# Attention masks in a two-block transformer kernel: one VectorE operation per head in place of identity products on TensorE

## The chip, the core and the metric

The kernel runs on one core of a Trainium2 chip. A core has five engines with an instruction queue each: TensorE (PE, matrix products; its weight loads are shown apart as PEld), VectorE (DVE), ScalarE (ACT), GpSimd (POOL) and SyncE (SP, which issues most transfers). Products land in PSUM; everything else works on SBUF. The metric is the device time of one execution in microseconds (us).

## What is computed

The reference is two models in sequence, each of depth 2, on one sequence of 256 tokens with 1024 channels, all float32. Each layer of the first has two feed-forward halves around a mixer with dilated-window attention (12 heads in three dilation groups) and stick-breaking attention (4 heads). Each layer of the second has a mixer of four branches (an attention with compressed, selected and windowed parts, a gated convolution, a pooling branch and a sliding-window attention with sinks), gates, and a feed-forward part. The change is in the softmax of the attentions. Cut to that:

```
# dilated window: key j is visible to query i if 0 <= i-j <= w and (i-j) % d == 0
s = einsum(q, k) * 64**-0.5
s = where(valid, s, -inf)
m = max(s);  p = exp(s - m);  o = (p @ v) / sum(p)

# banded attention (second model): window of 128 with sinks, or causal without
s = where(mask, einsum(q, k) * 64**-0.5, -1e30)
m = maximum(max(s), sink);  e = exp(s - m)
p = e / (sum(e) + exp(sink - m));  o = p @ v
```

## The kernel before

The 256 tokens are two tiles of 128 rows (t = 0, 1). All large products are done in three passes of a high and a low half of each operand; the low half of each weight chunk is made by VectorE (`wl`, line L111) and the high half by ScalarE (`wh`, L110), from chunks that SyncE loads. The products of such a chunk with activations stand in helper lines L184 to L186.

The program is written in order, layer by layer, but a scheduler places the instructions: it takes them by priority and by planned costs, puts independent ones into the gaps, and fixes one order per engine before the kernel runs. So gate products of the same mixer (`gate`, results `gt` at L955) are found between the attention's instructions, and the steps of the convolution (`conformer`, L911 and L914, 30 taps on each of four channel blocks) run on VectorE among the attention's.

First block, `attend1`: for each tile, heads are taken in pairs of `js`, and each keeps the scores of its dilation groups side by side in one PSUM bank of up to 512 columns (one group of 384 columns for t = 0, two of 512 and 256 for t = 1). A mask bank starts with a product of the identity (`identb`, bf16) and the additive mask `dilm` (0 or -1e30), L436; the score products of queries and keys (`qk`) of 64 rows each, L443, add to it. VectorE takes the maximum over the bank (L446), `probs` scales it (L454), ScalarE takes the exponential out of PSUM into an SBUF tile `e` with the sum beside it (L458), VectorE divides (L466), TensorE transposes (`transposed`, L155), and the value products follow (L488). The stick-breaking part keeps its own identity product (L499) in both kernels.

Second block, `attn`: called for the sliding-window attention (`window` true, with sinks) and twice for the causal one, for each tile and layer, always for 8 heads. For t = 0 a bank holds 4 heads of 128 columns, for t = 1 2 heads of 256. Identity products with the mask `swm` start each bank: L567 for t = 0, L569 for the window at t = 1, L571 for the causal case at t = 1, where only the second half of the columns needs one. Score products L578, then:

```
V.tensor_reduce(mx[:, sl], pv, op=OP.max, axis=AX.X)      # L584
V.tensor_scalar(ng[:, sl], mx[:, sl], -0.125, None, ...)  # L586, or L588 and L589 with sinks
S.activation(ev[:, i], pv[:, i], AF.Exp, bias=ng[...], scale=0.125, accum_out=dn[...])  # L593, per head
V.reciprocal(f[:, hh], dn[:, hh])                         # L602
V.tensor_tensor(ev, ev, f[...], op=OP.mult)               # L606
```

`turned` transposes the probabilities (L155) and copies them (L612, L614); L625 multiplies by the values. PSUM has two rings of four banks, `lin` and `aux`; scores, transposes and value products share `aux`. The SBUF tiles `e` come from a ring of 18. The masks are loaded once by GpSimd's queue at the start (`load_consts`).

Of the kernel before, what the change touches and what calls it, by code (L numbers as in the profile page):

```python
# [10 lines left out]
BF16 = mybir.dt.bfloat16  # L11
AF = mybir.ActivationFunctionType
# [13 lines left out]
def body(tc, ctx, I, C, out, upto=99):  # L26
# [35 lines left out]
    def const(name, shape, dt=F32):  # L62
        t = cp.tile(list(shape), dt, tag=name, name=name)
        pending.append((t, C[name]))
        return t
# [17 lines left out]
    G.memset(half, -0.5)  # L83
    dilm = [const(f"dilm{t}", [P, 3, (t + 1) * P], BF16) for t in range(2)]
    sbm = const("sbm", [P, P], BF16)
    swm = const("swm", [P, 2 * P], BF16)
    rope1 = [const(f"rope1_{t}", [P, 32]) for t in range(2)]
    rope2 = [const(f"rope2_{t}", [P, 128]) for t in range(2)]
    ntri = const("ntri", [P, P])
# [151 lines left out]
    def kouter(xts, w, nk, done, late=0):  # L241
# [3 lines left out]
        for b in range(2):  # L245
# [16 lines left out]
                go(1, c)  # L262
            done(1, b, ps[1])

    def square(src):

        junk = unit("junk", BF16, 1024)[:, :src.shape[-1]]
        m = stat()
        S.activation(junk, src, AF.Square, scale=1.0 / 32.0, accum_out=m)
        return m  # L270
# [127 lines left out]
    def attend1(qkn, vs):  # L398
        QT = [None, None]
        oTs = []  # L400
        for t in range(2):
# [19 lines left out]
            def qk(h, isk, tt):  # L421
                b = (h // 2) + (6 if isk else 0)
                o = (h % 2) * 64
                return QT[tt][b // 8][o:o + 64, (b % 8) * P:(b % 8 + 1) * P]
# [4 lines left out]
            def scores(js):  # L429

                r = [([], stat(4), stat(4)) for _ in js]
                for gi, gs in enumerate(groups):
                    n = len(gs) * nk * P
                    pss = [aux_ps()[:, :n] for _ in js]
                    for ps in pss:
                        nc.tensor.matmul(ps, identb, dilm[t][:, gs[0]:gs[-1] + 1, :].rearrange("p g k -> p (g k)"),  # L436
                                         start=True, stop=False)
                    for gg in gs:
                        for kt in range(nk):
                            c0 = ((gg - gs[0]) * nk + kt) * P  # L440
                            for ps, j in zip(pss, js):
                                h = gg * 4 + j
                                nc.tensor.matmul(ps[:, c0:c0 + P], qk(h, False, t), qk(h, True, kt), start=False,  # L443
                                                 stop=(gg == gs[-1] and kt == nk - 1))
                    for ps, (ps_l, mx, sm) in zip(pss, r):
                        V.tensor_reduce(mx[:, gi:gi + 1], ps, op=OP.max, axis=AX.X)  # L446
                        ps_l.append(ps)
                return r

            def probs(j, ps_l, mx, sm):  # L450

                if len(groups) == 2:
                    V.tensor_tensor(mx[:, 0:1], mx[:, 0:1], mx[:, 1:2], op=OP.max)
                V.tensor_scalar(mx[:, 2:3], mx[:, 0:1], -0.125, None, op0=OP.mult)  # L454
                es = []
                for gi, gs in enumerate(groups):
                    e = unit("e")[:, :len(gs) * nk * P]
                    S.activation(e, ps_l[gi], AF.Exp, bias=mx[:, 2:3], scale=0.125, accum_out=sm[:, gi:gi + 1])  # L458
                    es.append(e)
                if len(groups) == 2:  # L460
                    V.tensor_add(sm[:, 0:1], sm[:, 0:1], sm[:, 1:2])
                V.reciprocal(sm[:, 2:3], sm[:, 0:1])
                pts = []
                for gi, (gs, e) in enumerate(zip(groups, es)):
                    n = len(gs) * nk * P
                    V.tensor_scalar(e, e, sm[:, 2:3], None, op0=OP.mult)  # L466
                    pt = transposed(blocks(e, n // P))
                    u = unit("pt")[:, :n]
                    if gi == 0:
                        V.tensor_copy(u, pt)  # L470
                    else:
                        S.activation(u, pt, AF.Copy)
                    for gg in gs:
                        for kt in range(nk):
                            c0 = ((gg - gs[0]) * nk + kt) * P
                            h = gg * 4 + j
                            pts.append((vs[kt][:, h * 64:h * 64 + 64], u[:, c0:c0 + P]))
                return pts
# [73 lines left out]
    def attn(t, qT, kTf, vf, window, po, first, last, gate=None, sink=None):  # L552


        nk = t + 1
        per = 4 if t == 0 else 2
        mx, ng, dn, f = stat(8), stat(8), stat(8), stat(8)
        es = {}

        def scores(h0):  # L560

            n = per * nk * P
            pvs = []
            for _ in range(2):
                pv = aux_ps()[:, :n].rearrange("p (h k) -> p h k", h=per)
                if t == 0:
                    nc.tensor.matmul(pv, identb, swm[:, None, P:].to_broadcast([P, per, P]), start=True, stop=False)  # L567
                elif window:
                    nc.tensor.matmul(pv, identb, swm[:, None, :].to_broadcast([P, per, 2 * P]), start=True, stop=False)  # L569
                else:  # L570
                    nc.tensor.matmul(pv[:, :, P:], identb, swm[:, None, P:].to_broadcast([P, per, P]), start=True, stop=False)  # L571
                pvs.append(pv)
            for i in range(per):
                for kt in range(nk):
                    for par, pv in enumerate(pvs):
                        h = h0 + 2 * i + par
                        q_ = qT[par * 64:par * 64 + 64, (h // 2) * P:(h // 2 + 1) * P]
                        nc.tensor.matmul(pv[:, i, kt * P:(kt + 1) * P], q_, kTf(kt, h), start=False,  # L578
                                         stop=(i == per - 1 and kt == nk - 1))
            r = []  # L580
            for par, pv in enumerate(pvs):
                hs = list(range(h0 + par, h0 + 2 * per, 2))
                sl = slice(h0 + par, h0 + par + 2 * per - 1, 2)
                V.tensor_reduce(mx[:, sl], pv, op=OP.max, axis=AX.X)  # L584
                if sink is None:
                    V.tensor_scalar(ng[:, sl], mx[:, sl], -0.125, None, op0=OP.mult)  # L586
                else:
                    V.scalar_tensor_tensor(mx[:, sl], mx[:, sl], 0.125, sink[:, sl], op0=OP.mult, op1=OP.max)  # L588
                    V.tensor_scalar(ng[:, sl], mx[:, sl], -1.0, None, op0=OP.mult)  # L589
                e = unit("e")[:, :n]  # L590
                ev = e.rearrange("p (h k) -> p h k", h=per)
                for i, h in enumerate(hs):
                    S.activation(ev[:, i], pv[:, i], AF.Exp, bias=ng[:, h:h + 1], scale=0.125, accum_out=dn[:, h:h + 1])  # L593
                r.append((sl, ev))
                for i, h in enumerate(hs):
                    es[h] = ev[:, i]
            hh = slice(h0, h0 + 2 * per)
            if sink is not None:
                V.tensor_tensor(f[:, hh], sink[:, hh], ng[:, hh], op=OP.add)
                S.activation(f[:, hh], f[:, hh], AF.Exp)  # L600
                V.tensor_add(dn[:, hh], dn[:, hh], f[:, hh])
            V.reciprocal(f[:, hh], dn[:, hh])  # L602
            if gate is not None:
                V.tensor_tensor(f[:, hh], f[:, hh], gate[:, hh], op=OP.mult)
            for sl, ev in r:
                V.tensor_tensor(ev, ev, f[:, sl][:, :, None].to_broadcast([P, per, nk * P]), op=OP.mult)  # L606

        def turned(g, kt):
            u = unit("pt")
            pt = transposed([es[4 * g + r][:, kt * P:(kt + 1) * P] for r in range(4)])  # L610
            if (g + kt) % 2 == 0:
                V.tensor_copy(u, pt)  # L612
            else:
                S.activation(u, pt, AF.Copy)  # L614
            return u

        us = {}
        for h0 in range(0, 8, 2 * per):
            scores(h0)
        for kt in range(nk):  # L620
            for g in range(2):
                us[g, kt] = turned(g, kt)
        for kt in range(nk):
            for g in range(2):
                nc.tensor.matmul(po[g * 64:(g + 1) * 64], vf(kt, g), us[g, kt], start=first and kt == 0,  # L625
                                 stop=last and kt == nk - 1)
# [495 lines left out]
def constants():  # L1122
# [23 lines left out]
        c[f"cmpm{t}"] = np.concatenate([add, ok], axis=1).astype(f)  # L1146
    c["sbm"] = np.where(q < k, 0.0, NEG).astype(f)
    c["ntri"] = np.where(q >= k, -1.0, 0.0).astype(f)
    c["swm"] = np.concatenate([np.where(k > q, 0.0, NEG), np.where(k <= q, 0.0, NEG)], axis=1).astype(f)
    row = np.arange(P)  # L1150
    c["hsel"] = ((2 * ((row // 16) % 4) + row // 64)[:, None] == np.array([0, 4, 1, 5, 2, 6, 3, 7])[None, :]).astype(f)
    cnt = np.stack([np.minimum(np.arange(T) + 1, w) for w in (2, 4, 8, 16)]).astype(f)
# [54 lines left out]
```

## Time and profile before

| | |
|---|---|
| median of 3 runs | 2146.33 us |
| lowest, highest | 2140.66, 2147.63 us |
| profiled execution | 2142.42 us |
| span of its trace | 2140.7 us |
| mean granted TensorE clock | 0.997 of full speed |

The rows of the trace below come from the one profiled execution. Its time is the device time; the span is from the first to the last instruction of the trace. A group of instructions shows its count, its busy time, the mean of one, and the idle time of the engine just ahead of it. A matmul's duration runs from its start to its last result, so neighbouring ones overlap; the distance from start to start says how long the engine is taken.

### The profile page before, as it was taken

The page shows a single profiled execution, that of the slowest core. Times are in us where ns is not written, and L with a number is a line of the kernel's source. Part 1 is how long each engine was busy: PE and PEld are TensorE (multiplying, and loading weights), DVE is VectorE, ACT ScalarE, POOL GpSimd, SP SyncE. Part 2 cuts the span into 40 slices and gives each one's busy share as a digit, 9 for nine tenths or more (in the row PEclk, how much of TensorE's full clock was granted, in tenths as well). Part 3 has the DMA queues.
Part 4 walks back from the last instruction along what each step waited for, and adds up shares of the span by engine and source line. Part 5 has one row for each costly group of instructions (what it writes and reads, how often), then busy time and mean ns, then how long its engine had stood idle before and what let it go on. Part 6 is the DMA issues. An engine that isn't in the chain of part 4 may idle for free.

```text
span 2140.7 us, 30396 instructions
## 1 busy us (share of the span) xinstructions
PE 2103.5 (98%) x11520; PEld 1760.2 (82%) x11520; DVE 1576.4 (74%) x2439; ACT 1159.0 (54%) x1786; POOL 34.2 (2%) x47
## 2 busy tenths in 40 slices
PE   7999999999999999999999999999999999999998
PEld 6888877888888887788887877779987877788997
DVE  6875466786677555577757999678966899777983
ACT  5554556554555455555545655556655564446652
POOL 0000000000000000000000000000000000000000
PEclk9999999999999999999999999999999999999999
DMA  8666534666666654366666743356656644265653
GB/s 257 202 188 184 191 117 145 190 189 195 189 188 187 190 187 142 121 185 187 187 189 186 225 129 118 121 183 201 187 191 190 213 149 139 88 195 177 187 177 119
DMA packets 250818, 373.81 MB, mean 175 GB/s; under 512 B 14768, under 2 KB 123696, under 8 KB 250672
## 3 DMA queue, kind: packets, MB, share of 16 engines
q1 hardware_dynamic: 250096, 371.48, 56.8%
q8 instruction: 90, 1.47, 0.3%
q0 software_dynamic: 576, 0.39, 0.1%
q14 instruction: 56, 0.46, 0.1%
HBM read 371.17 MB, written 1.05 MB: 174 GB/s over the span
## 4 chain that ended last, share of the span: by engine, by line
PE 88%; DVE 7%; ACT 1%; issue 1%; DMA 1%; POOL 1%; SPq 0%; POOLq 0%; DVEq 0%; ACTq 0%
PE lin L186 15%; PE lin L185 15%; PE lin L184 15%; PE lin L218 15%; PE lin L219 8%; PE aux L155 3%; PE lin L205 3%; PE lin L206 3%; PE lin L204 3%; DVE cy L914 2%; DVE wl L111 2%; PE aux L625 1%; PE aux L578 1%; DMA raw<-in_w_in_dram 1%; PE aux L443 1%
## 5 line engine op out<-in xcount | busy, mean ns | idle before, releaser
L111 DVE TENSOR_TENSOR wl<-raw,wh 128x1024 fp32r<-128x1024 f32 (+1 forms) x688 | 835.1, 1217 | 393.4 <-ACT wh L110 386.1
L110 ACT ACTIVATE wh<-raw 128x1024 fp32r<-128x1024 f32 (+1 forms) x688 | 722.2, 1055 | 522.6 <-PE lin L186 277.3
L218 PE MATMUL lin<-x,wh 128*128 128x512 f32 x1408 | 494.8, 396 | 0.0
L219 PE MATMUL lin<-x,wl 128*128 128x256 f32 x1408 | 394.4, 280 | 0.0
L185 PE MATMUL lin<-wl,x 128*128 128x512 f32 (+2 forms) x896 | 348.2, 389 | 1.9 <-DVE wl L111 1.9
L184 PE MATMUL lin<-wh,x 128*128 128x512 f32 (+2 forms) x896 | 349.0, 390 | 0.0
L186 PE MATMUL lin<-wh,x 128*128 128x512 f32 (+2 forms) x896 | 346.7, 388 | 1.0 <-DVE rs L1105 0.8
L218 PEld LDWEIGHTS lin<-x,wh 128*128 128x128 f32 x1408 | 264.7, 188 | 62.4
L219 PEld LDWEIGHTS lin<-x,wl 128*128 128x128 f32 x1408 | 266.0, 189 | 0.5 <-DVE wl L111 0.4
L186 PEld LDWEIGHTS lin<-wh,x 128*128 128x128 f32 x896 | 168.7, 188 | 40.8 <-issue 5.2
L185 PEld LDWEIGHTS lin<-wl,x 128*128 128x128 f32 x896 | 168.7, 188 | 37.3 <-DVE wl L111 3.0
L184 PEld LDWEIGHTS lin<-wh,x 128*128 128x128 f32 x896 | 168.6, 188 | 36.5 <-issue 4.3
L186 PE MATMUL lin<-wh,lo 128*128 128x512 f32 x480 | 188.6, 393 | 0.4 <-DVE lo L147 0.4
L184 PE MATMUL lin<-wh,hi 128*128 128x512 f32 x480 | 187.3, 390 | 0.0
L185 PE MATMUL lin<-wl,hi 128*128 128x512 f32 x480 | 187.0, 390 | 0.0
L205 PE MATMUL lin<-x,wh 128*128 128x256 f32 x576 | 163.2, 283 | 0.0
L206 PE MATMUL lin<-x,wl 128*128 128x256 f32 x576 | 163.0, 283 | 0.0
L204 PE MATMUL lin<-x,wh 128*128 128x256 f32 x576 | 163.0, 283 | 0.0
L205 PEld LDWEIGHTS lin<-x,wh 128*128 128x128 f32 x576 | 110.6, 192 | 0.1
L204 PEld LDWEIGHTS lin<-x,wh 128*128 128x128 f32 x576 | 110.6, 192 | 0.1
L206 PEld LDWEIGHTS lin<-x,wl 128*128 128x128 f32 x576 | 110.6, 192 | 0.0
L225 ACT ACTIVATE su<-lin 128x256 f32<-128x256 f32 x176 | 65.4, 375 | 76.5 <-PE lin L219 76.5
(308 smaller groups left out, 2662.2 us busy)
## 6 DMA issues: line engine op xcount, KB each, us to landing
raw<-in_ffn_w_up_dram SPq DMA_DIRECT2D x168, 512.0 KB, 3.9
raw<-in_ffn_w_down_dram SPq DMA_DIRECT2D x132, 512.0 KB, 3.7
raw<-in_w_in_dram SPq DMA_DIRECT2D x132, 512.0 KB, 4.3
raw<-in_ffn_w_gate_dram SPq DMA_DIRECT2D x88, 512.0 KB, 3.8
raw<-in_w_gate_dram SPq DMA_DIRECT2D x64, 512.0 KB, 4.1
raw<-in_w_branch_dram SPq DMA_DIRECT2D x32, 512.0 KB, 4.2
raw<-in_w_out_dram SPq DMA_DIRECT2D x16, 512.0 KB, 4.5
raw<-in_nsa_cmp_w_dram SPq DMA_DIRECT2D x16, 512.0 KB, 4.5
```

The costliest lines, as they stand in the source:

```text
L110: S.activation(wh, raw, AF.Copy)
L111: V.tensor_sub(wl, raw, wh.bitcast(F32))
L155: nc.tensor.transpose(p[:, i * P:(i + 1) * P], s, ident)
L184: nc.tensor.matmul(ps, xt.h[k], w[0], start=start, stop=False)
L185: nc.tensor.matmul(ps, xt.h[k], w[1], start=False, stop=False)
L186: nc.tensor.matmul(ps, xt.l[k], w[0], start=False, stop=stop)
L204: nc.tensor.matmul(o, wh, xh, start=k == 0 and i % 2 == 0, stop=False)
L205: nc.tensor.matmul(o, wh, xl, start=False, stop=False)
L206: nc.tensor.matmul(o, wl, xh, start=False, stop=k == 7 and i % 2 == 1)
L218: nc.tensor.matmul(o, wh, x, start=k == 0, stop=False)
L219: nc.tensor.matmul(o[:, :T], wl, x[:, :T], start=False, stop=k == 7)
L225: S.activation(u[:, i * T:(i + 1) * T], p[:, T:], AF.Copy)
```

## The change

The masks are no longer added on TensorE. The first score product of a bank now starts it. A new helper `masked` adds the mask to the scores, writes the sum to the SBUF tile `e`, and takes the maximum, in one VectorE operation: per bank in `attend1`, per head in `attn`. The exponential then reads `e` and writes it in place. `swm` doubles to four blocks of 128 columns (earlier keys, own keys, zeros, own keys), so that each case finds its mask as one slice.

```
-    swm = const("swm", [P, 2 * P], BF16)
+    swm = const("swm", [P, 4 * P], BF16)
+    def masked(out, ps, mask, mx):
+        V.tensor_tensor_reduce(out, ps, mask, 1.0, NEG, OP.add, OP.max, mx)
...
-                    for ps in pss:
-                        nc.tensor.matmul(ps, identb, dilm[t][:, gs[0]:gs[-1] + 1, :].rearrange("p g k -> p (g k)"),
-                                         start=True, stop=False)
...
-                                nc.tensor.matmul(ps[:, c0:c0 + P], qk(h, False, t), qk(h, True, kt), start=False,
-                                                 stop=(gg == gs[-1] and kt == nk - 1))
+                                nc.tensor.matmul(ps[:, c0:c0 + P], qk(h, False, t), qk(h, True, kt),
+                                                 start=(gg == gs[0] and kt == 0), stop=(gg == gs[-1] and kt == nk - 1))
                     for ps, (ps_l, mx, sm) in zip(pss, r):
-                        V.tensor_reduce(mx[:, gi:gi + 1], ps, op=OP.max, axis=AX.X)
-                        ps_l.append(ps)
+                        e = unit("e")[:, :n]
+                        masked(e, ps, dilm[t][:, gs[0]:gs[-1] + 1, :].rearrange("p g k -> p (g k)"), mx[:, gi:gi + 1])
+                        ps_l.append(e)
...
-                    e = unit("e")[:, :len(gs) * nk * P]
-                    S.activation(e, ps_l[gi], AF.Exp, bias=mx[:, 2:3], scale=0.125, accum_out=sm[:, gi:gi + 1])
+                for gi, e in enumerate(es):
+                    S.activation(e, e, AF.Exp, bias=mx[:, 2:3], scale=0.125, accum_out=sm[:, gi:gi + 1])
...
+        mask = swm[:, 3 * P:] if t == 0 else swm[:, :2 * P] if window else swm[:, 2 * P:]
...
-                if t == 0:
-                    nc.tensor.matmul(pv, identb, swm[:, None, P:].to_broadcast([P, per, P]), start=True, stop=False)
-                elif window:
-                    nc.tensor.matmul(pv, identb, swm[:, None, :].to_broadcast([P, per, 2 * P]), start=True, stop=False)
-                else:
-                    nc.tensor.matmul(pv[:, :, P:], identb, swm[:, None, P:].to_broadcast([P, per, P]), start=True, stop=False)
...
-                        nc.tensor.matmul(pv[:, i, kt * P:(kt + 1) * P], q_, kTf(kt, h), start=False,
+                        nc.tensor.matmul(pv[:, i, kt * P:(kt + 1) * P], q_, kTf(kt, h), start=(i == 0 and kt == 0),
                                          stop=(i == per - 1 and kt == nk - 1))
...
-                V.tensor_reduce(mx[:, sl], pv, op=OP.max, axis=AX.X)
+                e = unit("e")[:, :n]
+                ev = e.rearrange("p (h k) -> p h k", h=per)
+                for i, h in enumerate(hs):
+                    masked(ev[:, i], pv[:, i], mask, mx[:, h:h + 1])
...
-                    S.activation(ev[:, i], pv[:, i], AF.Exp, bias=ng[:, h:h + 1], scale=0.125, accum_out=dn[:, h:h + 1])
+                    S.activation(ev[:, i], ev[:, i], AF.Exp, bias=ng[:, h:h + 1], scale=0.125, accum_out=dn[:, h:h + 1])
```

## Rows read from the trace of the kernel before

**Rows 1.** The page: busy time by engine, and VectorE in 40 slices.

```profile
PE 2103.5 (98%) x11520; PEld 1760.2 (82%) x11520; DVE 1576.4 (74%) x2439; ACT 1159.0 (54%) x1786; POOL 34.2 (2%) x47
...
DVE  6875466786677555577757999678966899777983
```

**Rows 2.** Busy time by stretch; columns: length, PE, PEld, DVE, ACT, POOL, clock, DMA.

```profile
840.00:905.00 65.00, 64.17 (x377) 48.52 (x374) 35.97 (x71) 39.23 (x64) 0.00 (x0) 1.00 0.37 110
...
1230.00:1260.00 30.00, 28.76 (x166) 21.27 (x165) 29.61 (x74) 18.60 (x50) 0.00 (x0) 1.00 0.36 118
...
1230.00:1350.00 120.00, 118.36 (x651) 86.19 (x649) 109.06 (x247) 63.64 (x156) 0.00 (x0) 1.00 0.37 114
...
1200.00:1204.00 4.00, 3.34 (x11) 2.95 (x12) 4.00 (x8) 3.58 (x8) 0.00 (x0) 0.57 0.66 174
```

**Rows 3.** Waits of PE and PEld, whole run: total us, times, longest.

```profile
PE aux L155 <- DVE e L606: 2.6, 6, 0.8
...
PEld aux L443 <- issue: 3.5, 14, 0.4
...
PEld aux L578 <- issue: 2.5, 10, 0.4
...
PEld L436 <- issue: 1.8, 8, 0.3
```

**Rows 4.** The masks' tiles: count, ns min/median/max, first and last start, forms.

```profile
L436 PE MATMUL aux<-dilm,identb x24: 273/331/389, 269.1 to 871.9; 128*128 128x384 bf16 x8, 128*128 128x512 bf16 x8, 128*128 128x256 bf16 x8
...
L571 PE MATMUL aux<-swm,identb x16: 272/282/283, 1317.9 to 1843.1; 128*128 128x256 bf16 x16
L567 PE MATMUL aux<-swm,identb x12: 379/379/390, 1231.4 to 1798.2; 128*128 128x512 bf16 x12
L569 PE MATMUL aux<-swm,identb x8: 379/379/389, 1250.1 to 1756.0; 128*128 128x512 bf16 x8
```

**Rows 5.** Timeline of PE: start, us from first start to last end, instructions merged.

```profile
276.14 0.50 PE L436 MATMUL aux<-dilm,identb 128*128 128x384 bf16 x2
...
285.05 0.38 PE L499 MATMUL aux<-sbm,identb 128*128 128x256 bf16 x2
...
1200.66 1.12 PE L155 MATMUL aux<-ident,kd 128*128 128x128 f32 x4 [2.21 <-DVE kd L550]
...
1231.38 0.59 PE L567 MATMUL aux<-swm,identb 128*128 128x512 bf16 x2
```

**Rows 6.** Groups by shape on ACT: busy us, mean ns, idle before and its releasers.

```profile
L146 ACT ACTIVATE hi<-su 128x512 fp32r<-128x512 f32 x44 | 27.1, 616 | 1.6 <-DVE su L343 1.6
...
L146 ACT ACTIVATE x<-aux 128x512 fp32r<-128x512 f32 x40 | 23.7, 596 | 11.9 <-PE aux L155 11.4
...
L593 ACT ACTIVATION_READ_ACCUMULATOR e<-aux,st 128x1 f32 x96 | 20.2, 210 | 0.0
...
L593 ACT ACTIVATE e<-aux,st 128x128 f32<-128x128 f32 (+1 forms) x96 | 39.1, 426 | 32.8 <-DVE st L586 25.3 <-DVE st L588 7.5
```

**Rows 7.** Timeline of DVE in second-block attention.

```profile
1283.99 1.28 DVE L584 TENSOR_REDUCE st<-aux 128x4 f32<-128x512 f32 x2
1285.19 0.16 DVE L586 TENSOR_SCALAR st<-st 128x4 f32<-128x4 f32 x1
1285.26 0.47 DVE L914 SCALAR_TENSOR_TENSOR cy<-cT,pm,cy 128x245 f32<-128x245 f32 x1
...
1315.38 0.29 DVE L895 TENSOR_TENSOR sc<-sc,st 128x128 f32<-128x128 f32 x1
1315.59 0.84 DVE L914 SCALAR_TENSOR_TENSOR cy<-cT,pm,cy 128x230 f32<-128x230 f32 x2
```

**Rows 8.** The convolution's split result: who writes it, who reads it.

```profile
L184 PE MATMUL lin<-wh,bhi x32: 389/389/393, 1402.2 to 1918.6; 128*128 128x512 f32 x32
...
L150 DVE SCALAR_TENSOR_TENSOR blo<-cy,bhi x2: 1224/1225/1226, 1370.1 to 1874.2; 128x1024 fp32r<-128x1024 f32 x2
```

**Rows 9.** DMA issues: KB each, median us to landing.

```profile
swm<-c_swm_dram POOLq DMA_DIRECT2D x1, 64.0 KB, 8.8
```

More of the change, by code (lines that the diff above doesn't have):

```diff
@@ L454, in probs @@
                 V.tensor_scalar(mx[:, 2:3], mx[:, 0:1], -0.125, None, op0=OP.mult)
-                es = []
-                for gi, gs in enumerate(groups):
-                    e = unit("e")[:, :len(gs) * nk * P]
-                    S.activation(e, ps_l[gi], AF.Exp, bias=mx[:, 2:3], scale=0.125, accum_out=sm[:, gi:gi + 1])
-                    es.append(e)
+                es = ps_l
+                for gi, e in enumerate(es):
+                    S.activation(e, e, AF.Exp, bias=mx[:, 2:3], scale=0.125, accum_out=sm[:, gi:gi + 1])
                 if len(groups) == 2:
@@ L564, in scores @@
             for _ in range(2):
-                pv = aux_ps()[:, :n].rearrange("p (h k) -> p h k", h=per)
-                if t == 0:
-                    nc.tensor.matmul(pv, identb, swm[:, None, P:].to_broadcast([P, per, P]), start=True, stop=False)
-                elif window:
-                    nc.tensor.matmul(pv, identb, swm[:, None, :].to_broadcast([P, per, 2 * P]), start=True, stop=False)
-                else:
-                    nc.tensor.matmul(pv[:, :, P:], identb, swm[:, None, P:].to_broadcast([P, per, P]), start=True, stop=False)
-                pvs.append(pv)
+                pvs.append(aux_ps()[:, :n].rearrange("p (h k) -> p h k", h=per))
             for i in range(per):
@@ L589, in scores @@
                     V.tensor_scalar(ng[:, sl], mx[:, sl], -1.0, None, op0=OP.mult)
-                e = unit("e")[:, :n]
-                ev = e.rearrange("p (h k) -> p h k", h=per)
                 for i, h in enumerate(hs):
-                    S.activation(ev[:, i], pv[:, i], AF.Exp, bias=ng[:, h:h + 1], scale=0.125, accum_out=dn[:, h:h + 1])
+                    S.activation(ev[:, i], ev[:, i], AF.Exp, bias=ng[:, h:h + 1], scale=0.125, accum_out=dn[:, h:h + 1])
                 r.append((sl, ev))
@@ L1148, in constants @@
     c["ntri"] = np.where(q >= k, -1.0, 0.0).astype(f)
-    c["swm"] = np.concatenate([np.where(k > q, 0.0, NEG), np.where(k <= q, 0.0, NEG)], axis=1).astype(f)
+    c["swm"] = np.concatenate([np.where(k > q, 0.0, NEG), np.where(k <= q, 0.0, NEG), np.zeros((P, P)),
+                               np.where(k <= q, 0.0, NEG)], axis=1).astype(f)
     row = np.arange(P)
```

## The prediction

> **What bounds the kernel now.** I read the page first. TensorE (PE) is busy 98% of the span, VectorE (DVE) 74% in the mean, but at 9 tenths in the slices around 1180 to 1340 us and 1710 to 1820 us [rows 1]. So the mean hides two regimes, and the busy time by stretch shows them: in first-block attention (840 to 905 us) PE is busy 64.17 of 65 us while DVE is free nearly half the time; in second-block attention (1230 to 1350 us) PE is busy 118.36 of 120 us at full clock and DVE 109.06, and between 1230 and 1260 us DVE has only 0.39 us free [rows 2]. Last, the list of waits: over the whole run PE waited for DVE's scaled probabilities (L606) 2.6 us, in 6 times [rows 3]. PE ends last everywhere near the change, because the scheduler fills the softmax latency with gate products. An instruction less on PE is therefore time less, as long as DVE, which also makes PE's low weight halves (L111), is not made late.
>
> **What leaves PE.** 60 identity products go: 8 + 12 + 8 of 512 columns, 8 of 384, and 8 + 16 of 256 [rows 4]. Their durations overlap with their neighbours', so I price them by pairs. Two of 512 columns take 0.59 us where one takes 0.38: 0.21 us each. Two of 384 take 0.50 against 0.33: 0.17. Two of 256 (the same product in L499, which stays) take 0.38 against 0.28: 0.10 [rows 4, 5]. Sum: 28 x 0.21 + 8 x 0.17 + 24 x 0.10 = 5.9 + 1.4 + 2.4 = 9.7 us. To that come gaps: the weight loads stood 1.8 us ahead of L436, 3.5 us ahead of L443 and 2.5 us ahead of L578 with nothing but issue in the way [rows 3]. The 1.8 us go with L436. Of the other 6.0 us the part remains where a score block still follows transposes or value products; I let up to half go. So PE saves 9.7 us by streaming alone and 9.7 + 1.8 + 3.0 = 14.5 at most; I take 11, nearer to the part that rows show directly. That these products merely stood in waits is a rival below.
>
> **What comes to DVE.** 36 maxima over several heads (L584, 512 columns) become one operation per head: in each layer three attentions of 8 heads in each of two tiles, 48 a layer and 96 in all, 48 of 128 and 48 of 256 columns. The 24 maxima of the first block (L446) become 24 operations of the same width. A DVE operation that writes both a sum and its maximum is in no row, so I bound it. What counts is start to start: two 512-column maxima hold DVE from 1283.99 to 1285.19 us, 0.60 each; a two-input operation of 128 columns is followed after 0.21 us; on the line between them 256 columns hold it 0.34 [rows 7]. Below, the maximum comes with the stream at no price: 48 x 0.21 + 48 x 0.34 - 36 x 0.60 = 10.1 + 16.3 - 21.6 = +4.8 us, and nothing in the first block. Above, the maximum is read out as ScalarE reads out its sum, in an instruction of 0.21 us [rows 6]: 120 x 0.21 = 25.2 more, +30.0 us. The nearest DVE row is the tiny operation, which the next one follows after 0.07 us (1285.19 to 1285.26) [rows 7]; with 0.08 to be a little above it the sum is 4.8 + 120 x 0.08 = +14.4 us: 2.4 + 48 x 0.08 = 6.2 in each layer of the second block and 1 in each of the first. I take this one.
>
> The cover for the 6.2 us is the convolution (L914), which DVE runs among the attention work: its split result is written from 1370.1 us and PE first loads it at 1402.2 us [rows 8], about 30 us of slack, and 10.94 of the 120 us are free besides [rows 2]. So I cost the throughput at nothing. If that cover is gone, or the convolution stands ahead of the new work in DVE's fixed order, the sum falls on PE (first rival).
>
> Latency is the second part. In a first-tile attention the maxima of both head groups took 2 x 0.60 = 1.2 us; eight operations of 0.21 + 0.08 take 2.3, so 1.1 later. In a second-tile step four of 0.42 take 1.7, so 0.5 later. What is late next is the exponential (L593), then L602, L606 and the transposes of L155 on PE, and behind those the gate products in PE's order. Most of it is filled with gate products; at the six places where PE waits for L606 already [rows 3] I add 0.3 to 0.4 us each: 2 us lost.
>
> **The rest.** ScalarE's 120 exponentials read SBUF instead of PSUM. The nearest rows, a 512-column copy from SBUF at 616 ns and one from PSUM at 596 [rows 6], put it at 0.02 us each, 2.4 us: nothing, hidden by the 32.8 us that ScalarE waits for DVE ahead of L593 [rows 6]; without that cover it would be 2.4 us on PE's transposes. Score banks come free after the DVE operation instead of after the exponentials, and the SBUF tile of the exponentials, one of 18, is taken as much earlier: both nothing, since no row has PE waiting long for either. The mask load on GpSimd's queue doubles from 64 KB, which landed in 8.8 us [rows 9], and is the last on that queue, 1200 us ahead of its reader at 1231 us [rows 5]: nothing, and some 9 us if it had to be waited for.
>
> [...]
>
> **Sum.** PE -11, waits +2: -9 us. The profiled execution took 2142.42 us, its span 2140.7 (the table above); -9 gives 2133.4. It lies 3.9 us under the median of the runs shown, 2146.33, and from that the same -9 gives 2137.
>
> **Rivals.**
>
> *DVE becomes the bound of attention (slower).* For it: 0.39 us free from 1230 to 1260 us [rows 2], and DVE's order is fixed when the kernel is built; if the new operation is longer than was planned for, convolution pieces and L111 behind it slip, and PE, also in order, waits at the next transpose. Against it: the slack of the convolution, and 120 operations are few beside 2439 [rows 1]. With nothing absorbed the sum is -11 + 14.4 = +3 us at my price and -11 + 30 = +19 at the upper one; it decides (+6.4) from 17.4 us that reach PE, that is from a read-out of 0.105 us with nothing absorbed. [...] 2149 to 2165 us; chance 0.15.
>
> *The products filled waits (no change).* For it: at 1231.38 us a mask pair runs directly behind the transposes of the queries [rows 5], whose copy to SBUF the score products need, so it may cost nothing there. If half the streamed time merely turns into waits, or DVE's 6 us a layer reach PE in part, -3 us remains: 2143 (2140 to 2150). Against it: PE has gate products at hand in almost every such gap. Chance 0.27.
>
> *More comes back.* Every gap that could go does, and no wait is added: -14.5 us, 2132 (2128 to 2132). Chance 0.08.
>
> **How the numbers follow.** The forecast, 2137 us with a range of its own of 2132 to 2140, has 0.50. The range 2128 to 2150 leaves out most of the first rival's 0.15 and little else. A difference under 0.3% (6.4 us) is about what a measurement of this kernel can't tell from no change. Faster by more: 0.48 of the forecast and 0.08 of the last case, 0.56. Within: 0.02 + 0.27 and a little of the first rival, 0.30. Slower: 0.14.
>
> **What would show it.** Right: PE has 60 matmuls fewer and its busy time falls by about 10 us; DVE's busy time rises by 10 to 30 us; the convolution ends later, still before 1402 us; PE's waits for L606 and L111 stay under 10 us. Wrong: DVE operations that hold the engine 0.5 us or more for 128 columns; a granted clock under 0.9 in attention; PE waiting for L111 or L606 by more than 10 us in all; or gate products in another order, so that time moves where the change is not.

## The result, and the profile after

The changed kernel takes 2118.72 us (median of 4 runs, 2113.38 to 2119.26); the kernel before took 2145.01 us beside it (4 runs, 2140.66 to 2147.63). The ratio is 0.9874, with an interval of 0.985 to 0.9897: 26 us faster. The forecast was 2137 us, with a range of 2128 to 2150: the sign was right, the size was not, and the time lies 9 us below the range.

The profiled execution took 2119.26 us, its span 2117.5. The page of the changed kernel, busy time by engine:

```profile
PE 2081.5 (98%) x11460; PEld 1752.2 (83%) x11460; DVE 1580.3 (75%) x2619; ACT 1164.2 (55%) x1786; POOL 34.2 (2%) x47
...
DVE  6875566777687555577857899878976899977983
```

Against [rows 1] PE has its 60 matmuls fewer and is busy 22.0 us less; its idle time stays where it was (2140.7 - 2103.5 = 37.2 us, now 36.0). So the 23 us of span came out of PE's busy time, and that is twice what the removed products were priced at. DVE has 180 instructions more and is busy only 3.9 us longer.

Where it happened is read by stage. A stage lies between two tiny GpSimd operations (`st<-st,half`), which the trace of every kernel here has at the same places of the program: the two attention stages of the first block and the two mixer layers of the second. Busy time in these four, before (columns as in [rows 2]):

```profile
203.50:386.40 182.90, 181.85 (x947) 143.88 (x947) 108.79 (x175) 98.50 (x144) 2.01 (x2) 1.00 0.49 152
757.50:940.50 183.00, 181.95 (x947) 143.88 (x947) 108.81 (x175) 98.37 (x144) 2.01 (x2) 1.00 0.49 153
1136.30:1433.30 297.00, 290.24 (x1506) 229.87 (x1505) 245.37 (x450) 157.79 (x285) 1.40 (x4) 0.99 0.52 162
1638.10:1938.40 300.30, 294.07 (x1520) 232.58 (x1519) 246.99 (x451) 158.36 (x286) 1.38 (x4) 0.99 0.52 162
```

and after:

```profile
206.40:385.30 178.90, 178.14 (x935) 142.23 (x934) 108.95 (x187) 98.48 (x145) 2.03 (x3) 1.00 0.49 156
758.50:937.50 179.00, 178.21 (x935) 142.30 (x935) 108.92 (x187) 98.52 (x144) 2.01 (x2) 1.00 0.50 156
1133.40:1421.20 287.80, 282.00 (x1488) 227.61 (x1487) 246.95 (x528) 159.87 (x286) 1.44 (x5) 0.99 0.55 167
1626.00:1915.60 289.60, 283.56 (x1502) 228.94 (x1501) 248.58 (x529) 160.59 (x286) 1.38 (x4) 1.00 0.54 168
```

The two first stages shorten by 4.0 us each, the two layers by 9.2 and 10.7: 28 us. The rest of the span, whose work is the same, took 1177.4 us before and 1182.3 after (1178 to 1182 in the kernels of the experiments), which is why the spans differ by 23 only. DVE's busy column hardly moves in any of the four. From here on kernels are compared by these four lengths, beside their medians.

**What the new operation costs DVE.** Groups by shape, the changed kernel (`aux` is a PSUM bank: VectorE reads the scores there itself, as ScalarE did before [rows 6], so not everything but the products works on SBUF):

```profile
L267 DVE CUSTOM_DVE_ANT_0 e<-aux,swm 128x256 f32<-128x256 f32 x48 | 18.5, 419 | 0.0
...
L267 DVE CUSTOM_DVE_ANT_0 e<-aux,swm 128x128 f32<-128x128 f32 x48 | 11.2, 289 | 0.2
...
L267 DVE DVE_READ_ACCUMULATOR2_ANT st<- 128x1 f32 x120 | 10.1, 85 | 0.0
```

The maximum is read out in an instruction of its own, 85 ns long, 120 of them: near the 0.08 us that the prediction took. But the timeline of DVE shows that it costs nothing:

```profile
1230.59 0.28 DVE L267 CUSTOM_DVE_ANT_0 e<-aux,swm 128x128 f32<-128x128 f32 x1
1230.80 0.08 DVE L267 DVE_READ_ACCUMULATOR2_ANT st<- 128x1 f32 x1
1230.80 0.28 DVE L267 CUSTOM_DVE_ANT_0 e<-aux,swm 128x128 f32<-128x128 f32 x1
1231.01 0.08 DVE L267 DVE_READ_ACCUMULATOR2_ANT st<- 128x1 f32 x1
...
1315.12 0.42 DVE L267 CUSTOM_DVE_ANT_0 e<-aux,swm 128x256 f32<-128x256 f32 x1
1315.46 0.09 DVE L267 DVE_READ_ACCUMULATOR2_ANT st<- 128x1 f32 x1
1315.46 0.42 DVE L267 CUSTOM_DVE_ANT_0 e<-aux,swm 128x256 f32<-128x256 f32 x1
```

The read-out starts at the same instant as the next operation. Start to start an operation of 128 columns takes 0.21 us with its read-out and one of 256 columns 0.34: the prediction's lower bound (+4.8 us in all), not its choice (+14.4). The 0.34 - 0.21 = 0.13 us for 128 columns more leave about 0.08 us of each operation that does not grow with the columns, an estimate from these two distances.

**What PE waits for.** List of waits, PE alone, the changed kernel:

```profile
PE aux L155 <- DVE e L601: 2.5, 2, 1.3
PE lin L185 <- DVE wl L111: 1.5, 2, 0.8
...
PE aux L572 <- DVE st L267: 0.8, 2, 0.4
PE aux L155 <- DVE e L466: 0.7, 2, 0.4
```

L601 is L606 of before: 2.5 us in 2 times, where it was 2.6 in 6 [rows 3]. The 2 us that were added there for latency didn't come; two other waits for DVE that the list of before doesn't have, for the new operation ahead of the next score products (L572) and for the scaled probabilities of the first block (L466), take 1.5 us together.

**Work that was not touched.** The value products of the second block (L625 before, L620 after) are the same 36 products, each with two records in the trace. Their group before:

```profile
L625 PE MATMUL aux<-pt,vv 128*64 128x512 f32 x72 | 25.5, 616 | 0.2 <-ACT pt L614 0.2
```

and after:

```profile
L620 PE MATMUL aux<-pt,vv 128*64 128x512 f32 x72 | 19.3, 612 | 0.0
```

The timeline of PE at the end of a layer, before:

```profile
1344.34 1.07 PE L625 MATMUL aux<-pt,vv 128*64 128x512 f32 x2
1345.35 0.50 PE L186 MATMUL lin<-wh,x 128*128 128x512 f32 x1
...
1347.81 1.07 PE L625 MATMUL aux<-pt,vv 128*64 128x512 f32 x2 [0.18 <-ACT pt L614]
1348.81 0.51 PE L186 MATMUL lin<-wh,x 128*128 128x512 f32 x1
...
1349.47 1.08 PE L625 MATMUL aux<-pt,vv 128*64 128x512 f32 x4
```

and after:

```profile
1339.74 2.06 PE L620 MATMUL aux<-pt,vv 128*64 128x512 f32 x8
```

The products of the two head groups, each with weights of 128*64, write the two halves of 64 rows of one result (`po`). One alone (x2) takes 1.07 us; two that stand next to each other (x4) take 1.08 us: they run side by side. In the kernel before, gate products and transposes (from L186 on) stood between the two products of this pair, and three pairs of nine in each layer are broken in such a way; after, none is. Six pairs at 1.0 us are the 6.2 us between 25.5 and 19.3. The change doesn't touch these products, and the prediction names them only as neighbours of the score products.

**The clock.** Near the end of the second layer of the kernel before, PE waited 0.46 us, and behind it the granted clock fell; the place in the timeline of PE, and busy time by stretch:

```profile
1865.73 0.84 PE L934 MATMUL aux<-ident,st 128*128 128x128 f32 x4 [0.46 <-POOL st L931]
```

```profile
1866.00:1870.00 4.00, 4.00 (x14) 3.24 (x14) 3.33 (x7) 0.79 (x1) 0.00 (x0) 0.57 0.00 0
```

With a granted clock of 0.57, (1 - 0.57) x 4 = 1.7 us of these 4 us are lost against full clock (an estimate from the two figures). At the same place of the program the changed kernel holds full clock, 1.00:

```profile
1847.00:1855.00 8.00, 8.00 (x47) 6.89 (x46) 6.33 (x11) 2.28 (x3) 0.70 (x1) 1.00 0.41 133
```

### The profile page after: what moved, and what is told of

It reads as the page before. It is cut to its first block, busy times and chain, and to the rows that moved or that the text cites. A ratio compares the mean times of both kernels' runs of the same rounds, so it can differ in the third digit from the quotient of the medians.

```text
span 2117.5 us, 30460 instructions
## 1 busy us (share of the span) xinstructions
PE 2081.5 (98%) x11460; PEld 1752.2 (83%) x11460; DVE 1580.3 (75%) x2619; ACT 1164.2 (55%) x1786; POOL 34.2 (2%) x47
## 4 chain that ended last, share of the span: by engine, by line
PE 89%; DVE 6%; ACT 2%; issue 1%; DMA 1%; POOL 0%; SPq 0%; POOLq 0%; DVEq 0%; ACTq 0%
PE lin L186 16%; PE lin L185 16%; PE lin L218 16%; PE lin L184 16%; PE lin L219 8%; PE aux L155 3%; PE lin L206 3%; PE lin L205 3%; PE lin L204 3%; DVE wl L111 2%; DVE cy L909 1%; ACT wh L110 1%; PE aux L620 1%; DMA raw<-in_w_in_dram 1%; PE aux L572 1%
## 5 line engine op out<-in xcount | busy, mean ns | idle before, releaser
L186 PE MATMUL lin<-wh,x 128*128 128x512 f32 (+2 forms) x896 | 347.1, 388 | 1.0 <-DVE rs L1100 0.8
L186 PEld LDWEIGHTS lin<-wh,x 128*128 128x128 f32 x896 | 168.7, 188 | 35.9 <-DVE rs L1100 1.6
L186 PE MATMUL lin<-wh,lo 128*128 128x512 f32 x480 | 188.5, 393 | 0.5 <-DVE lo L147 0.5
```

Of the source, the lines that this page charges most:

```text
L186: nc.tensor.matmul(ps, xt.l[k], w[0], start=False, stop=stop)
```

## The experiments

Theory A at the start: the time came from three things, the removed products, the order of PE's remaining work (pairs above all), and score banks that come free at the masked operation instead of after the exponentials. Rivals: B, that the products explain all; C, that it is the earlier release; D, that DVE's work is in fact paid on PE. From e1 on each was timed beside the kernel before, both on the same chip (2143 to 2144 us); the first two rows are the result above. The table has the median, the ratio, and the lengths of the four stages from the profiled execution. For the two layers the time lost to the clock, worked out as above, is already taken off and stands in the last column, since such dips came and went between executions.

| kernel | median us | ratio, interval | 1st block, 2 stages | layer 0 | layer 1 | clock, us |
|---|---|---|---|---|---|---|
| before | 2145.01 | 1 | 182.9, 183.0 | 295.3 | 298.7 | 3.4 |
| changed | 2118.72 | 0.9874 [0.985, 0.9897] | 178.9, 179.0 | 286.0 | 289.6 | 1.7 |
| e1 no mask | 2132.8 | 0.9946 [0.9933, 0.996] | 180.1, 180.1 | 291.5 | 295.8 | 0 |
| e2 both masks | 2132.08 | 0.9945 [0.9932, 0.9957] | 181.6, 181.7 | 290.1 | 292.8 | 5.1 |
| e3 held banks | 2128.24 | 0.9923 [0.9912, 0.9935] | 180.4, 180.5 | 290.0 | 293.9 | 1.7 |
| e4 before, tied | 2138.37 | 0.9972 [0.9964, 0.998] | 182.9, 182.9 | 291.9 | 294.8 | 1.7 |
| e5 doubled, tied | 2146.6 | 1.0018 [1.0008, 1.0029] | 178.2, 178.3 | 295.4 | 300.0 | 18.8 |
| e6 by bank, tied | 2131.56 | 0.9949 [0.9934, 0.9964] | 178.8, 179.0 | 290.4 | 293.8 | 6.8 |
| e7 changed, tied | 2120.25 | 0.9892 [0.9879, 0.9905] | 178.8, 178.9 | 287.8 | 291.9 | 1.7 |
| e8 held, tied | 2122.89 | 0.9909 [0.9896, 0.9923] | 180.4, 180.5 | 287.3 | 290.9 | 0 |
| e9 first block only | 2134.36 | 0.9956 [0.9942, 0.997] | 178.9, 179.0 | 295.9 | 297.8 | 0 |
| e10 second block only | 2125.78 | 0.9915 [0.99, 0.993] | 182.9, 182.9 | 287.2 | 290.1 | 1.7 |
| e11 no mask, tied | 2119.61 | 0.9889 [0.9872, 0.9905] | 180.1, 180.2 | 286.0 | 289.8 | 1.7 |

**e1: no mask on any engine.** The kernel before without its identity products, the masks left out altogether.

```diff
-                    for ps in pss:
-                        nc.tensor.matmul(ps, identb, dilm[t]..., start=True, stop=False)
...
-                if t == 0:
-                    nc.tensor.matmul(pv, identb, swm[:, None, P:]..., start=True, stop=False)
...
+                pvs.append(aux_ps()[:, :n].rearrange("p (h k) -> p h k", h=per))
```

> The kernel before without its identity products, and with no mask added anywhere (the masks are left out of the result); maxima over the bank and exponentials out of PSUM stay as they were. Theory A: the fall of 26 us has three parts: the mask products with their gaps on PE (about 12.5 us), value products of the second block that stand in pairs again (6 pairs were apart, 1 us each), and a clock dip that goes away (about 3 to 5 us). In this build 6 pairs are still apart, so A expects value products at about 12 us a layer as before and a time 12 to 20 us under before, 2125 to 2133. Rival B: taking the mask work off PE is all there is; then this run shows the whole fall, 2117 to 2121.

2132.8 us. Rival B falls: with the products gone and nothing put in their place, less than half of the gain is there. By stages the products are worth 2.8 + 2.9 + 3.8 + 2.9 = 12.4 us. Six pairs are broken in its order, as before.

**e2: masks on both engines.** The changed kernel with the identity products kept as well, so that every mask is added twice.

```diff
+                    for ps in pss:
+                        nc.tensor.matmul(ps, identb, dilm[t]..., start=True, stop=False)
...
-                pvs.append(aux_ps()[:, :n].rearrange("p (h k) -> p h k", h=per))
+                (the identity products of before)
```

> The changed kernel with the identity products put back on PE, so that masks are added on both engines; score banks still come free after the VectorE operation. In this build no pair is apart. Theory A: only the pairs and perhaps the dip come back, 6 to 10 us under before, 2135 to 2140, with value products at about 9.2 us a layer. Rival B: the same PE work as before and more on VectorE, so 2143 to 2155. Rival C: the early release of the banks is the main cause; then most of the fall stays, 2120 to 2130.

2132.08 us, under theory A's range and just over rival C's: PE has all its mask products back, DVE has all the new work, and 12 us of the 26 remain. So nearly half of the gain has nothing to do with the removed products. The first-block stages are 1.3 us shorter than before, the layers 5.2 and 5.9 us, and no pair is broken.

**e3: the bank held as before.** Masks on DVE, but written back into the PSUM bank, from which the exponentials read.

```diff
-                        masked(e, ps, dilm[t]..., mx[:, gi:gi + 1])
+                        masked(ps, ps, dilm[t]..., mx[:, gi:gi + 1])
...
-                    masked(ev[:, i], pv[:, i], mask, mx[:, h:h + 1])
+                    masked(pv[:, i], pv[:, i], mask, mx[:, h:h + 1])
...
-                    S.activation(ev[:, i], ev[:, i], AF.Exp, ...
+                    S.activation(ev[:, i], pv[:, i], AF.Exp, ...
```

> The changed kernel with the VectorE operation writing its sum back into the score bank, so that the bank is held until the exponential has read it, as before the change. In this build 4 pairs are apart. Theory A: the mask work is gone, 4 us of the pairs are lost: 4 to 8 us over the changed kernel, 2122 to 2128. Rival B: the same as the changed kernel, 2117 to 2121. Rival C: most of the fall is lost, over 2132.

2128.24 us, just over theory A's range and under rival C's. The order that came out breaks four pairs, so release and pairs are mixed here; e8 separates them.

**e4: the pairs alone.** The kernel before, with one tiny DVE operation per pair that makes the first product's operand wait for the second's, so that both products of a pair become ready together. It adds zero times one value to another.

```diff
                 us[g, kt] = turned(g, kt)
+            a, b = us[0, kt][:, 0:1], us[1, kt][:, 0:1]
+            V.scalar_tensor_tensor(a, b, 0.0, a, op0=OP.mult, op1=OP.add)
```

> The kernel before with one tiny VectorE operation more per pair of value products (18 in all), which makes both products of a pair ready at the same time; the result is unchanged. No pair is apart in this build. Theory A: value products fall from about 12.2 to about 9.2 us a layer, and the time by about 6 us, 2136 to 2142. If pairs do not matter on PE: 2143 to 2149.

2138.37 us, in the middle of theory A's range. The timeline of PE in this kernel, at the end of a layer, has two whole pairs:

```profile
1346.54 1.94 PE L627 MATMUL aux<-pt,vv 128*64 128x512 f32 x8
1348.41 0.50 PE L186 MATMUL lin<-wh,x 128*128 128x512 f32 x1
```

The group of the value products is at 19.0 us here, where it was at 25.5:

```profile
L627 PE MATMUL aux<-pt,vv 128*64 128x512 f32 x72 | 19.0, 615 | 0.0
```

The first block doesn't move, the two layers give 3.4 and 3.9 us: six pairs at 1.0 us and a little more. The pairs are shown as a cause.

**e8: held banks, with tied pairs.** The kernel of e3 with the two lines of e4.

> The masks are added on VectorE as in the changed kernel, but the masked scores are written back into the PSUM bank, which stays taken until the exponentials have read it, and the two value products of a pair are tied so that they stand next to each other, as they do in the changed kernel. What separates it from the changed kernel is then only when a score bank comes free. Theory A (the removed products, the pairs and the earlier release of the banks each have a share): 2123 to 2128 us, about 7 us over the changed kernel, and 1 to 5 us under the same kernel without the tie (2128.2), since two to four broken pairs go. Rival C (the earlier release is worth nothing of its own, it only happened to keep the pairs together): 2117 to 2121 us. In the trace, by theory A, TensorE waits again for the exponential of the stick-breaking weights (0.8 us in a first-block layer).

2122.89 us, just under theory A's range. Against the changed kernel the first-block stages are 1.5 us longer each, and the layers 1.3 each; against the changed kernel with the same tie (e7) the layers are 0.5 and 1.0 us shorter. So the earlier release is worth about 3 us, in the first block, and nothing that can be told in the second. The edit changes one thing more than when a bank comes free: a masked operation that writes into PSUM takes longer on DVE (444 ns in the mean for 256 columns, where it took 419), and so does its read-out, 146 ns where it took 85:

```profile
L267 DVE DVE_READ_ACCUMULATOR2_ANT st<- 128x1 f32 x120 | 17.5, 146 | 0.0
```

For the first block this matters little: e1 and e11, which hold the banks and have no masked operation, take 180.1 and 180.2 us there, 1.2 over the changed kernel. The list of waits of e8 names the place in the first block:

```profile
PE aux L528 <- ACT sw L520: 1.6, 2, 0.8
```

The kernel before has this wait too (its L527, 1.6 us in 2 times); the list of the changed kernel doesn't. It is half of the 3 us. Another 1.0 is in the score products of the stick-breaking part, 64 rows each, which touch no mask of this change; their group by shape in e8 and in the changed kernel:

```profile
L509 PE MATMUL aux<-qt,qt 64*128 64x128 f32 x16 | 3.4, 310 | 0.0
```

```profile
L508 PE MATMUL aux<-qt,qt 64*128 64x128 f32 x16 | 2.4, 310 | 0.0
```

**e7: the changed kernel, tied.**

> The changed kernel with the 18 tiny VectorE operations that tie the pairs of value products. Its pairs already stand together, so if the tie itself costs and gives nothing it takes the time of the changed kernel, 2116 to 2121 us. If the tie gained in the kernel before by anything else than the pairs (another order), it should gain here too: 2111 to 2115 us.

2120.25 us: its interval of 0.9879 to 0.9905 overlaps with that of the changed kernel. By the median the tie gives nothing where no pair is broken, so what it gave in e4 is the pairs. But its layers are 1.8 and 2.3 us longer than the changed kernel's: a new build is a new order, and with the same work on PE its layers came out 4 us longer.

**e9 and e10: one block each.** The edits of the first block alone (around L448 of the changed kernel), and those of the second alone (around L581).

> The change in the first block alone: the masks of its attention are added on VectorE, those of the second block stay identity products as before. Theory A by stages (the products and the banks in the first block, the rest in the second): the two first-block attention stages shorten by 4 us each as they do in the changed kernel and nothing else moves, 2134 to 2138 us beside 2143 to 2145, with six broken pairs of value products as before. Rival B (the first block has products only, 2.6 us a layer): 2138 to 2141 us.

> The change in the second block alone: the first block keeps its 24 identity products, and no pair of value products is broken. Theory A: the whole of the rest, 18 us in two layers (removed products 7.4, pairs 6, clock and waits the remaining 4 to 5), 2124 to 2130 us, and together with the run of the first block alone the two savings add up to that of the changed kernel (24 to 28 us). Rival: they don't add up by over 4 us, that is, the order of one block reaches into the other.

2134.36 and 2125.78 us beside 2143.25: 8.9 and 17.5 us, together 26.4, the changed kernel's 26.3. The stages agree: in e9 the first block's shorten by 4.0 us each and the layers move by under 1, in e10 only the layers shorten. So the order of one block reaches into the other by no more than 2 us: the layers of e10 together are 1.7 us longer than the changed kernel's. Both times lie within theory A's ranges.

**e11: no mask, tied pairs.** The kernel of e1, which leaves the masks out, with the two lines of e4.

> The kernel before without any mask on any engine (it leaves the masks out of the softmax attentions), maxima over whole banks and exponentials from PSUM as before, pairs tied. It has every product away and the pairs, no new work on VectorE, and the banks held to the exponential. Theory A: the time of the version with masks on VectorE, held banks and tied pairs (2122.9) less what the masked operations cost, that is 2120 to 2125 us: the new operations cost TensorE at most 2 us. Rival D (their time or latency comes through by more): 2112 to 2118 us.

2119.61 us, just under theory A's range. Against e8, which differs from it in the masked operations alone, it is 3.3 us shorter by the median and 3.0 by the stages (2.4 of it in the layers); against the changed kernel its layers are the same, 286.0 and 289.8 us beside 286.0 and 289.6. So what the masked operations cost PE lies between nothing and about 3 us, and the prediction's 2 us are not refuted by it.

Products (12.4 us by e1) and pairs (7.3 by e4) make 19.7, and without the clock the four stages of e11 are 23.8 us shorter than before: 4 us are in neither run. They don't hang on having both. The layers of e7, which has both, are 14.3 us shorter than before, where e1 and e4 add up to 14.0; and those of e2, where every product is still in place, are 11.1 us shorter, 3.8 more than the pairs give. Five builds have no mask product and no broken pair in the second block (changed, e7, e8, e10, e11), and their two layers take 575.6, 579.7, 578.2, 577.3 and 575.8 us. So some 4 us lie between builds whose work on PE is the same in these layers.

**e5: twice the DVE work.** The changed kernel, tied, with each masked operation issued twice.

```diff
         V.tensor_tensor_reduce(out, ps, mask, 1.0, NEG, OP.add, OP.max, mx)
+        V.tensor_tensor_reduce(out, ps, mask, 1.0, NEG, OP.add, OP.max, mx)
```

> The changed kernel with every masked operation issued twice with the same operands, pairs tied: 120 more operations and 120 more read-outs on VectorE, by the rows of the changed kernel 18.5 + 11.2 + 12.4 + 10.1 = 52 us of VectorE, some 19 of it in each second-block layer and 7 in each first-block layer. Theory A (VectorE's work is covered, only the 0.4 to 0.7 us of latency shows at a few places): 2119 to 2127 us. Rival D (VectorE sets the pace where it is busy at 9 tenths, so its time falls on TensorE): 2145 to 2171 us. Between them the cover is partly used up, and the part that comes through is the answer.

2146.6 us, 26 us over e7 and 3 over the kernel before: rival D at its lower edge, though 52 us was too much for the work added. With overlaps counted once it is 38 us, 27 of it in the second block. The first block swallows its share (178.2 and 178.3 us, even shorter). The second doesn't: in the profiled execution, the longest of its runs (2152.04 us), the layers lose 7.6 + 8.1 us against e7, in waits, and 17 to the clock. From its list of waits:

```profile
PE aux L155 <- DVE e L602: 11.6, 6, 2.3
```

and busy time by stretch around one of them:

```profile
1332.00:1336.00 4.00, 1.95 (x10) 1.20 (x8) 2.65 (x10) 2.69 (x10) 0.00 (x0) 1.00 0.00 0
1336.00:1340.00 4.00, 1.90 (x8) 1.25 (x7) 4.00 (x10) 0.71 (x4) 0.00 (x0) 0.59 0.00 0
1340.00:1344.00 4.00, 4.00 (x16) 2.52 (x14) 3.13 (x9) 1.09 (x2) 0.00 (x0) 0.56 0.02 4
```

PE is idle half of the first 8 us; the granted clock is 0.59 in the second stretch and 0.56 in the third.

**e6: addition and maximum apart.** The changed kernel, tied, with one addition over a bank and one maximum over it in the second block.

```diff
-                for i, h in enumerate(hs):
-                    masked(ev[:, i], pv[:, i], mask, mx[:, h:h + 1])
+                V.tensor_tensor(ev, pv, mask[:, None, :].to_broadcast([P, per, nk * P]), op=OP.add)
+                V.tensor_reduce(mx[:, sl], ev, op=OP.max, axis=AX.X)
```

> The changed kernel, but in the second block one addition of the mask over a whole bank (512 columns) and one maximum over it, instead of an operation per head with its read-out; pairs tied. VectorE gets 72 operations of 512 columns in place of 96 with 96 read-outs (by rows of about 0.6 us and of 0.29, 0.42 and 0.085 us: 43 us in place of 38), and in a first-tile step the latency is about 2.4 us for two banks as before. Theory A (VectorE covered): the time of the changed kernel, 2117 to 2122 us. If the form of the operation matters on TensorE's path (that the maximum comes in the same pass): over 2124 us.

2131.56 us, 11 us over e7: theory A's part on DVE, that its time is covered, falls. The sums of DVE's time, overlaps counted once, are 21.6 + 21.4 us for the two forms where the changed kernel has 26.6 with its read-outs: 16 us more, 8 a layer. From its list of waits:

```profile
PE aux L924 <- ACT sq L920: 5.4, 2, 2.7
```

the place in the timeline of PE:

```profile
1353.40 1.95 PE L924 MATMUL aux<-avg,sq 128*128 128x1 f32 x16 [2.72 <-ACT sq L920]
```

and busy time by stretch there:

```profile
1352.00:1356.00 4.00, 2.60 (x18) 2.24 (x18) 2.61 (x5) 1.06 (x1) 0.31 (x1) 0.91 0.21 58
1356.00:1362.00 6.00, 5.07 (x14) 3.94 (x14) 4.06 (x7) 1.06 (x1) 1.23 (x1) 0.50 0.39 139
```

The convolution comes late, PE waits 2.7 us for the squares of its statistics, and the clock stands at 0.50 for 6 us behind it. The slack that this used up is seen in the timeline of DVE: the last piece of the convolution and the subtraction of its mean, in the kernel before

```profile
1339.15 0.46 DVE L914 SCALAR_TENSOR_TENSOR cy<-cT,pm,cy 128x226 f32<-128x226 f32 x1
1356.81 1.21 DVE L921 TENSOR_TENSOR cy<-cy,aux 128x1024 f32<-128x1024 f32 x1
```

and in the changed kernel

```profile
1348.83 0.45 DVE L909 SCALAR_TENSOR_TENSOR cy<-cT,pm,cy 128x226 f32<-128x226 f32 x1
...
1350.39 1.22 DVE L916 TENSOR_TENSOR cy<-cy,aux 128x1024 f32<-128x1024 f32 x1
```

Before, 17.2 us passed between the two; after, 1.1 us. PE's products of the mean, the first on PE to read the last piece, are in the kernel before

```profile
1353.80 1.89 PE L920 MATMUL aux<-cy,avg 128*128 128x256 f32 x8
```

and in the changed kernel, the last two of them,

```profile
1349.33 0.70 PE L915 MATMUL aux<-cy,avg 128*128 128x256 f32 x2
```

That is 14.2 us after the last piece is done (1339.61 us), and 0.05 us after it (1349.28 us). By this reading the changed kernel stands just at the point where DVE begins to set the end of the layer.

## Why the prediction was wrong

**The step that failed** is "So PE saves 9.7 us by streaming alone and 9.7 + 1.8 + 3.0 = 14.5 at most; I take 11, nearer to the part that rows show directly." As a price of the removed products it holds: e1 measures 12.4 us, between the two ends. It was wrong as the whole of what PE can save. It takes the rest of PE's order as given, and that order is made anew when the kernel is built. The runs put in its place, with the clock taken off (26.4 us in the four stages):

- 12.4 us, the products alone (e1);
- 7.3 us, six pairs of value products that are no longer broken (e4; 6.5 us of it in the busy time of their group);
- about 4 us that are in neither of the two (e11 against e1 and e4). The changed kernel and e11 have them, e2 too, with the products in place, and e7 hardly any, with both; so they belong, as far as these runs tell, to the order that a build comes out with, and which gaps between smaller products they are stays open. As large a part of the 12.4 and the 7.3 may be of this kind, since each is one build;
- 2.4 us, the first-block stages below those of e11, where the bank is held (1.2 each; against e8, which has the masked operations, 1.5 each).

Besides, one dip of the clock is gone in the profiled execution, 1.7 us.

**"Score banks come free after the DVE operation instead of after the exponentials ... nothing"** was wrong by 2.4 to 3 us in the first block, where one wait of 0.8 us a layer hung on it; in the second nothing can be told.

**The DVE term** was mis-sized: +14.4 us taken, +3.9 in the busy time; the lower bound of 4.8 was the right row. The read-out has the length that was taken, 85 ns beside 0.08 us, and it runs beside the next operation: both start at 1230.80 us in the timeline above.

**"So I cost the throughput at nothing"** came out right, for a wrong reason. The 30 us of slack were read between the convolution's split result and its first load on PE [rows 8]. The convolution's first reader in PE's order is the group mean and the squares behind it, where the slack was 14 us, of which nothing is left. The prediction's own +14.4 us would hardly have been covered in full: e6 has 16 us more DVE work in the second block than the changed kernel and takes 11 us longer, waits and clock together. So the first rival's mechanism exists, with its place at another consumer; it stayed away because the operation was cheaper than taken.

**The 2 us of waits for L606** didn't come there; the wait is 2.5 us in 2 times, and 1.5 us of new waits for DVE stand elsewhere. In the doubled kernel it is 11.6.

**The rivals.** That the products filled waits is refuted by e1. "More comes back" had the sign of the error, but its 14.5 us were a bound on gaps beside the removed products. The last sentence of the list of what would make the prediction wrong, gate products in another order, "so that time moves where the change is not", is what happened: the order was named as a risk and given no price.

Why the pairs were split before and not after is only argued. It isn't the removal of the products: in e1 six pairs are broken as before, in e3, with masked operations and held banks, four, and in e2 and e10, with masked operations and early release, none. What is argued: each product waits for its own copy of the transposed probabilities, and where the two copies land apart the order has a ready gate product to put between. That the tie alone closes the pairs agrees with it.

## What to carry to other kernels

Where the order of an engine is built anew from the whole program, the price of an edit is not that of the removed instructions: look in the trace for places where the order of before is bad (products that could run side by side and don't, a wait next to a filler), since an edit can close or open them, and try such a place alone, as two lines did here. Build the same work in more than one way before a small difference is given a cause: here builds with the same work on PE differed by 4 us in two layers. When an engine's time is costed at nothing, find the first reader of what it delays, in the order of the engine that bounds, and doubly so where a wait is followed by a lower clock, as in e6 (0.50 for 6 us). A DVE operation's price is its distance from start to start in a row of equal ones, not its duration: here 0.21 us beside 0.28 for 128 columns, and 0.34 beside 0.42 for 256.

## What the hardware showed that was not expected

- Two value products, with weights of 128*64 and into the two halves of one result, take 1.08 us when they stand next to each other, and one alone 1.07 us.
- The accumulator's read-out, 85 ns, starts together with the next DVE operation, and the 0.21 us from one 128-column operation to the next hold it. Where the masked operation writes into PSUM (e8), the read-out takes 146 ns.
- A wait of 2.7 us on PE is followed by 6 us at a granted clock of 0.50 in e6; by the estimate above the dips cost 1.7 us a layer in the kernel before, 3.4 a layer in e6, and 8.5 and 10.2 in the two layers of e5. A wait of 2 or 3 us didn't bring one each time. In the kernel before, the wait of 2.21 us at 1200.66 us was followed by 0.57 [rows 2, 5], and one of 2.20 us for the same transposes in the second layer by full clock:

```profile
1706.10 0.66 PE L155 MATMUL aux<-ident,kd 128*128 128x128 f32 x4 [2.20 <-DVE kd L550]
```

```profile
1695.00:1710.00 15.00, 12.41 (x80) 10.49 (x79) 13.46 (x25) 10.13 (x17) 0.00 (x0) 1.00 0.79 241
```

In e1 this second wait is 3.04 us long, and the clock stays full too (0 us in the table's last column). So the 1.7 us stand for the dip behind one such wait, and are not the price of each.
